# A two-block transformer kernel: the loop over further tiles goes to the very end, a shift's products beside an earlier stage, and a bias strip's copy behind the gates

## The chip, the cores and the metric

The kernel runs on one core of one Trainium2 chip. The metric is the device time of one execution in microseconds (us), as the median of several runs. The engines are TensorE (PE, with its weight loads as PEld), VectorE (DVE), ScalarE (ACT), GpSimd (POOL) and SyncE (SP), which issues most of the DMAs.

## The reference, cut to what matters

Two transformer blocks run one after the other on x (512 tokens, 1024 features). The parts that the change touches:

```
# first block
h = rms_norm(x, g_mix);  proj = h @ w_in             # conv, q, k, v, index, gates
y_a = short_conv_mixer(c_b, c_c, c_x) @ w_branch_a
logits = q k / 8 + rel_bias[rel_bucket(t - s)]       # the bias strip: 8 heads
merged = sigmoid(g_a) * y_a + sigmoid(g_b) * y_b
x = x + merged @ w_out
x = x + (silu(h2 @ w_ffn_gate) * (h2 @ w_ffn_up)) @ w_ffn_down
# second block
sh1, sc1, gt1, sh2, sc2, gt2 = split(silu(c) @ ada_w + ada_b)
h = rmsnorm(x, norm1_g) * (1 + sc1) + sh1            # sh1: the shift
z = h @ w_in                                         # first 768 columns: the latents
...
h = rmsnorm(x, norm2_g) * (1 + sc2) + sh2
x = x + gt2 * hierarchical_moe(h, ...)               # 32 experts, 2 of 8 in 1 of 4 groups
return rmsnorm(x, final_norm_g)
```

## The kernel before

Weights stream from HBM in blocks of 128 x 1024 (512 KB). `dense` (L351 on) loads a block on SP's queue (L333), splits it into a high part on ACT (L338) and a low part on POOL (L339), and multiplies on PE: three products per block of 128 features, high by high, high by low, low by high (L347). One output block takes 24 matmuls for 8 feature blocks, and 33 for the 11 feature blocks of a half of the down products. Nine buffers hold raw, high and low blocks. The order on each engine is made by a planner that simulates the program; a queue then works in that order. A `keep` pins an instruction to program order, and `issue_after` makes one wait for another.

First block. The index scores and the top-k (DVE, L566 and L567) run beside the convolution's products w_cv. A table `bd` of 8 x 640 biases is made (L598, written by ACT's queue) and spread into the strip `bt`, 8 x 128 x 512 values or 2 MB in DRAM, by one DMA (L645): each of the 128 rows is the table shifted by one. The strips `st` of the heads are fetched from bt in the attention (L766). Then come the gates: w_ga (sigmoid on ACT, L653), w_ya (times the gate, `mA`, on DVE, L660) and w_gb, whose rest is interleaved with the attention.

The feed-forward part runs in two halves. Each has 22 gate-up products (`w_gu`) and 8 down products (`w_dn`). Beside them the vectors of the second block are made: `ada` (L704) streams ada_w through DVE, one step a product in the first half, two in the second, where they run out after 12 of the 22 products. The latents' `shift` (six of them, one a product) loads a block of w_lat, multiplies it with the shift vector on DVE (L905, and seven times L907), sums over partitions by a product of one column on PE (L909) and copies it to `shc` (L910). They run beside the down products of the second half, as do the rotary tables and the masks.

The experts. Tokens are gathered into tiles; 16 tiles of two experts each are worked through in the order `seq`, and a 17th tile of 64 rows takes what did not fit. `finish` adds a tile's rows to `acc` in DRAM by an indirect DMA; the last two tiles (`NCH` = 2) stay on chip as `yh`, `yl` with one-hot matrices `oh`, and `place` adds them by products (L1799) to `fin`, the blocks read back from acc (L1789). If still more tiles are needed, `loop` works them one by one; their number `ntl` is data, and the loop runs from 1 to ntl, so for ntl = 1 it makes no pass. In the execution shown it makes none. It stands in the last step, after `hidden` of the 17th tile and before its `turn` and `finish`; at its place (L1730) every engine tests ntl, jumps, and then waits on the semaphores of all engines and queues before it goes on. At the end come the sums of squares (`sq`, ACT, L1821), the products with g (`tg`, POOL, L1824), the inverse root (`ms`, `rs`, DVE, L1825 and L413 to L421), the scaling and the output.

Of the kernel before, what the change touches and what calls it, by code (L numbers as in the profile page):

```python
# [11 lines left out]
F32 = mybir.dt.float32  # L12
F32R = mybir.dt.float32r
I32 = mybir.dt.int32
ACT = mybir.ActivationFunctionType
ALU = mybir.AluOpType
# [3 lines left out]
P = 128  # L20
S = 512
D = 1024
NB = 4
# [5 lines left out]
NL = 6  # L29
# [20 lines left out]
FM = "ppss"  # L50
# [23 lines left out]
GA1 = (0, 0, 0, 1, 0, 1, 0, 1, 1, 0)  # L74
NW = 9
NCH = 2
LOOP = 16
LF = True
NX = 18
NR = 8  # L80
# [5 lines left out]
AD = (1, 1, 2, 2)  # L86
# [152 lines left out]
def build(tc, A, out, taps=None):  # L239
    nc = tc.nc  # L240
# [11 lines left out]
    V, G = nc.vector, nc.gpsimd  # L252
    TT, STT, TS = V.tensor_tensor, V.scalar_tensor_tensor, V.tensor_scalar
    act = nc.scalar.activation
# [14 lines left out]
    def blk(name, dt=F32):  # L269
        if late:  # L270
            return late[0].tile([P, S], dt, tag="t", bufs=3, name=name)
        pool, tag = (lpool, "b") if name in LATE else (epool, "c") if name in EARLY else (epool, "d") if name in MID else (lpool, "t")
        return pool.tile([P, S], dt, tag=tag, bufs=BUFS[tag], name=name)

    def psum(tag, name=None):
        return psp.tile([P, S], F32, tag=tag, bufs={"mm": 3, "lg": 2, "tp": 2, "po": 1}[tag],
                        name="p" + (name or tag))

    def raw_tile(name="raw", dt=F32):
        return wpool.tile([P, D], dt, tag="w", bufs=NW, name=name)  # L280
# [50 lines left out]
    def wload(src, n):  # L331
        raw = raw_tile()
        nc.sync.dma_start(raw[:, :n], src)  # L333
        return raw
# [110 lines left out]
    class Ssq:  # L445
# [4 lines left out]
        def add(self, t, scale=1.0, pin=False):  # L450
            sq = blk("sq" if self.acc else "acc")
            i = act(sq, t, ACT.Square, scale=scale)
            if pin:
                keep(i)
            if self.acc is None:
                self.acc = sq
            else:
                self.eng.tensor_tensor(self.acc, self.acc, sq, ALU.add)
# [9 lines left out]
    def x_tile(name):  # L468
        return xpool.tile([P, D], F32, tag="x", bufs=4, name=name)
# [169 lines left out]
    def beside(i):  # L639
        scores.run(SC[3])  # L640
        if not scores.ts:
            tops.run(TOP)

    go(dense("w_cv", DB, h, ev_cv), beside)
    nc.sync.dma_start(bt, bass.AP(tensor=bd.tensor, offset=bd.offset + 127,  # L645
                                    ap=[[640, 8], [-1, P], [1, S]]))


    gts = {}
# [3 lines left out]
        act(t, ps, ACT.Sigmoid, bias=vcol("b_gate", m))  # L653
        gts[m] = t

    mA = []

    def ev_ya(m, ps):
        t = blk("mA")
        TT(t, ps, gts[m], ALU.mult)  # L660
        mA.append(t)

    ga, ya = dense("w_ga", DB, h, ev_ga), dense("w_ya", 4, chl, ev_ya)
    for _ in range(NGA):
        next(ga)
        tops.run(3)
        next(ya)
        tops.run(1)
    tops.run(99)

    gd = {}
# [227 lines left out]

    shc = kpool.tile([P, NL], F32, name="shc")  # L900

    def shift(c):
        raw = wload(A["w_lat"][c].rearrange("p m k c -> p (m k c)"), D)
        t = blk("t")[:, :P]
        TS(t, raw[:, :P], adac[:, :1], None, ALU.mult)  # L905
        for k in range(1, DB):
            STT(t, raw[:, k * P:(k + 1) * P], adac[:, k:k + 1], t, ALU.mult, ALU.add)  # L907
        ps = psum("lg", "shift")
        mm(ps[:, :1], t, one1[:, :1])  # L909
        act(shc[:, c:c + 1], ps[:, :1], ACT.Copy)  # L910

    shifts = Tasks(*[(shift, c) for c in range(NL)])


    gs1 = kpool.tile([P, 8], F32, name="gs1")
# [3 lines left out]
    for half in range(2):  # L919
        hid = []  # L920
        st = {}

        def ev_gu(m, ps):
            t = blk("t")
            if m % 2 == 0:
                TT(t, ps, r, ALU.mult)
                act(t, t, ACT.Silu)  # L927
                G.tensor_tensor(t, t, r, ALU.mult)  # L928
                st["g"] = t
            else:  # L930
                TT(t, ps, st["g"], ALU.mult)
                a = pair_of("h" if len(hid) < NH else "h1" if len(hid) < NH1 else "hid")
                split(t, *a)
                hid.append(a)

        if half == 0:
            with soon(1):
                r = rstd_of(ssq.done(), out=blk("m2"))
        if half == 0:
            keep(act(cact, vcol2("c", 0, 8), ACT.Silu))  # L940
            keep(G.tensor_copy(trib, cst[:, 256:384]))
            G.tensor_copy(tri2[:, :32], cst[:32, 256:288])
            G.tensor_tensor(tri2[:, 32:], cst[:32, 256:288], cst[:32, :32], ALU.add)
            G.tensor_copy(moeb, moec[:, 88:328])
            G.memset(oneb, 1.0)
        go(dense("w_gu", DB, h, ev_gu, src=A["w_gu"][half * 22:(half + 1) * 22]),
           lambda i: adas.run(AD[2 * half]))

        def ev_d(m, ps):
            TT(x[m], ps, x[m], ALU.add)  # L950
            if half:
                a = pair_of("xg")
                split(x[m], *a, scale=gs1[:, m:m + 1])
                xg.append(a)
                s1.add(x[m])
                s2.add(x[m], scale=vcol("g_final", m))

        if half:
            STT(gs1, adac[:, 8:16], 1.0, vcol2("norm1_g", 0, 8), ALU.add, ALU.mult)
            TT(gs1, gs1, vcol("g_final", 0, 8), ALU.mult)  # L960
            rt = rope_tables()
            mk = masks()
        go(dense("w_dn", 11, hid, ev_d, src=A["w_dn"][half]),
           lambda i: shifts.run(1) if half else adas.run(AD[2 * half + 1]))


    KQ = 96
# [719 lines left out]
    def weights(i, after=True):  # L1687
        g = seq[i]
        if g == 16:
            wes[i] = further(0)  # L1690
            return
        more(upto[g] - len(we), after)
        wes[i] = [[we[n, j] for j in range(3)] for n in (2 * g, 2 * g + 1)]
# [28 lines left out]
        ohs.append(oh)  # L1722
        ys.append((yh, yl))

    def loop():
        for j in range(LOOP + 1, 17):
            weights(j, LF)

        ntl = nc.values_load(ei[0:1, 16:17], min_val=1, max_val=16)
        with tc.For_i(1, ntl) as t:  # L1730
            st = mr[0].tile([P, 4], F32, name="lsl")[:, :3]

            nc.sync.dma_start(slots[16 * P:].rearrange("(g p) c -> p g c", p=P), slt[:, 16:])
            nc.sync.dma_start(st[:64], slots[bass.ds(16 * P + 64 * t, 64)])
            ix = mr[0].tile([P, 1], I32, name="lix")
            V.tensor_copy(ix[:64], st[:64, 0:1])
            w = further(t)
            xg = gather(xgb[0], ix, 64)
            scaled(64, xg, st)
            down(w, turned(64, hidden(w, features(64, xg, xtb), st)), yb[0])  # L1740
            add(64, yb[0], ix, acc)

    def rows_in_place(i):
        xts[i] = features(size(i), xgb[i % NQ], xtb)
# [16 lines left out]
    for i in range(17):  # L1761
        if i not in wes:
            weights(i)
        if i == 15:
            weights(16)
            gfr = xgb[i % NQ]
            keep(nc.sync.dma_start(gfr, A["gfin"].broadcast_to([P, D])))
        hss[i] = hidden(wes[i], xts.pop(i), slt[:, seq[i]], (lambda: turn(i - 1)) if i else None)
        if i < 16:
            rows_in_place(i + 1)  # L1770
        if i < 15:
            scaled(size(i + 2), xgb[(i + 2) % NQ], slt[:, seq[i + 2]])
        if i:
            finish(i - 1)
        if i == 0:
            further_tiles(further_slots())
        if i == LOOP:
            loop()
    turn(16)
    finish(16)  # L1780

    if LOOP == 17:
        loop()


    fin = []
    for b in range(NB):
        fin.append(mr[0].tile([P, D], F32, tag="we", bufs=NR, name="fin"))
        (nc.scalar if FQ and b % 2 else nc.sync).dma_start(fin[b], acc[b * P:(b + 1) * P])  # L1789
# [21 lines left out]
    for b in range(2):  # L1811
        for q in range(2):
            placed(b, q, 0)

    for g in FGR:
        n = len(g)
        ms = mr[0].tile([P, n], F32, tag="ms%d" % n, bufs=2, name="ms")
        tg = {}
        for j, b in enumerate(g):
            place(b)  # L1820
            act(x_tile("sq"), fin[b], ACT.Square, accum_out=ms[:, j:j + 1])  # L1821
            if FM[b] != "s":
                tg[b] = mr[0].tile([P, D], F32, tag="we", bufs=NR, name="tg")
                (G if FM[b] in "pq" else V).tensor_tensor(tg[b], fin[b], gfr, ALU.mult)  # L1824
        TS(ms, ms, 1.0 / D, EPS, ALU.mult, ALU.add)  # L1825
        r = rsqrt4(ms, lambda: mr[0].tile([P, n], F32, tag="rs%d" % n, bufs=6, name="rs"))
        for j, b in enumerate(g):
            t, c = fin[b], r[:, j:j + 1]
            if FM[b] == "s":
                STT(t, t, c, gfr, ALU.mult, ALU.mult)  # L1830
            elif FM[b] in "qw":
                t = tg[b]
                TS(t, t, c, None, ALU.mult)
            else:
                t = tg[b]
                act(t, t, ACT.Copy, scale=c)
            (nc.scalar if FQ and b % 2 else nc.sync).dma_start(out[b * P:(b + 1) * P], t)
# [16 lines left out]
```

## Time and profile before

| | |
|---|---|
| runs | 1366.8, 1363.75, 1368.21 us |
| median | 1366.8 us |
| profiled execution | 1365.68 us, of which the span from the first to the last instruction 1363.9 us |
| mean granted clock of TensorE | 0.964 |
| busy share | PE 93%, PEld 69%, DVE 62%, ACT 40%, POOL 47% |
| moved by DMA | 209.19 MB, 153 GB/s in the mean |

All rows come from one profiled execution. Its own time is the reference for sums of durations; the median of the runs is the reference for the result. A matmul's end is modelled: in the timeline the rows of PE overlap a little.

### The profile page before, as it was taken

How to read it: one execution, taken by the hardware profiler on the slowest of the kernel's cores; microseconds unless marked ns; L12 is line 12 of the kernel's file. 1: busy time of each engine (PE TensorE's matmuls, PEld its weight loads, DVE VectorE, ACT ScalarE, POOL GpSimd, SP SyncE). 2: the span in 40 equal slices, each digit the busy share in tenths (PEclk: the TensorE clock that was granted, in tenths of full speed). 3: DMA queues.
4: the chain of work that ended last, by engine and by line, in shares of the span. 5: the costliest groups of instructions: out<-in, count | busy, mean ns of one | idle time of the engine just before them, and what ended most of it. 6: DMA issues, size and time to landing. Idle time of an engine off the chain costs nothing. (4 is left out here: it accounts for less than half of the span.)

```text
span 1363.9 us, 16404 instructions
## 1 busy us (share of the span) xinstructions
PE 1263.6 (93%) x5818; PEld 946.5 (69%) x5818; DVE 845.9 (62%) x1490; ACT 544.8 (40%) x902; POOL 645.7 (47%) x365
## 2 busy tenths in 40 slices
PE   6798999999999999999998999899979999679985
PEld 5576887777888778777886777778855587445432
DVE  5857885543758443377249676979977753554424
ACT  4443236566333332222323454233376532244422
POOL 4514447454547554454745755346734263123311
PEclk9898999999999999999999999899989999879987
DMA  5214233223245544575333322234430069989983
GB/s 171 80 49 147 103 99 125 99 95 125 93 137 201 202 156 149 185 244 193 118 116 112 118 93 78 71 124 131 131 108 16 24 236 356 347 302 288 273 306 134
DMA packets 70403, 209.19 MB, mean 153 GB/s; under 512 B 9635, under 2 KB 14427, under 8 KB 70320
## 3 DMA queue, kind: packets, MB, share of 16 engines
q1 hardware_dynamic: 61456, 193.81, 41.4%
q0 software_dynamic: 4048, 8.01, 2.5%
q10 hardware_dynamic: 4816, 6.31, 1.3%
q8 instruction: 46, 0.75, 0.2%
q14 instruction: 37, 0.30, 0.1%
HBM read 195.06 MB, written 21.61 MB: 159 GB/s over the span
## 5 line engine op out<-in xcount | busy, mean ns | idle before, releaser
L339 POOL TENSOR_TENSOR wl<-raw,wh 128x1024 fp32r<-128x1024 f32 (+2 forms) x180 | 420.0, 2335 | 418.7 <-ACT wh L338 350.0
L338 ACT ACTIVATE wh<-raw 128x1024 fp32r<-128x1024 f32 (+2 forms) x183 | 183.3, 1003 | 297.8 <-DMA raw<-in_w_dn 59.3
L347 PE MATMUL pw_gu<-xg,wh 128*128 128x512 f32 x704 | 168.9, 391 | 0.0
L347 PEld LDWEIGHTS pw_gu<-xg,wh 128*128 128x128 f32 x704 | 131.4, 188 | 31.3 <-issue 2.5
L704 DVE SCALAR_TENSOR_TENSOR ad<-raw,cact,ad 128x512 f32<-128x512 f32 x84 | 89.0, 1107 | 37.1 <-DMA raw<-in_ada 37.1
L347 PE MATMUL pw_dn<-h,wh 128*128 128x512 f32 x352 | 88.6, 397 | 0.7 <-ACT wh L338 0.7
L347 PE MATMUL pw_cv<-h,wh 128*128 128x512 f32 x320 | 81.0, 405 | 8.0 <-ACT wh L338 5.0
L1048 DVE SCALAR_TENSOR_TENSOR ptaps<-u,vec,ptaps 128x511 f32<-128x511 f32 (+28 forms) x116 | 85.8, 739 | 3.6
L347 PE MATMUL pw_gu<-xg,wl 128*128 128x512 f32 x352 | 87.7, 390 | 0.0
L1639 PE MATMUL plg<-we,xt 128*64 128x256 f32 (+1 forms) x528 | 75.0, 406 | 9.2 <-DMA we<-in_we 6.0
L347 PEld LDWEIGHTS pw_cv<-h,wh 128*128 128x128 f32 x320 | 62.2, 196 | 23.6 <-ACT wh L338 5.9
L347 PEld LDWEIGHTS pw_dn<-h,wh 128*128 128x128 f32 x352 | 66.1, 190 | 15.6 <-ACT wh L338 1.2
L347 PEld LDWEIGHTS pw_gu<-xg,wl 128*128 128x128 f32 x352 | 65.9, 188 | 13.8
L1639 PEld LDWEIGHTS plg<-we,xt 128*64 128x64 f32 (+1 forms) x528 | 39.8, 136 | 40.2 <-issue 13.5
L347 PE MATMUL pw_gb<-h,wh 128*128 128x512 f32 x256 | 64.3, 394 | 0.0
L347 PE MATMUL pw_ga<-h,wh 128*128 128x512 f32 x256 | 62.3, 391 | 0.0
L347 PEld LDWEIGHTS pw_ga<-h,wh 128*128 128x128 f32 x256 | 47.7, 188 | 10.3 <-issue 0.8
L347 PEld LDWEIGHTS pw_gb<-h,wh 128*128 128x128 f32 x256 | 47.4, 188 | 9.2
L735 DVE TENSOR_SCALAR e<-e,ri 128x512 f32<-128x512 f32 (+2 forms) x64 | 49.0, 767 | 1.7
L928 POOL TENSOR_TENSOR t<-t,m 128x512 f32<-128x512 f32 x22 | 33.3, 1514 | 34.7 <-ACT t L927 32.7
L1600 POOL DMA_INDIRECT xg<-htok,sidx x17 | 17.2, 1012 | 67.2 <-ACT xt L1629 50.1
L733 ACT ACTIVATE e<-e,mx 128x512 f32<-128x512 f32 (+2 forms) x64 | 40.7, 637 | 20.1 <-DVE mx L776 13.2
(463 smaller groups left out, 2504.4 us busy)
## 6 DMA issues: line engine op xcount, KB each, us to landing
we<-in_we SPq DMA_DIRECT2D x99, 512.0 KB
raw<-in_ada SPq DMA_DIRECT2D x48, 512.0 KB
raw<-in_w_gu SPq DMA_DIRECT2D x44, 512.0 KB
raw<-in_w_cv SPq DMA_DIRECT2D x20, 512.0 KB
raw<-in_w_ga SPq DMA_DIRECT2D x16, 512.0 KB
raw<-in_w_gb SPq DMA_DIRECT2D x16, 512.0 KB
raw<-in_w_o SPq DMA_DIRECT2D x16, 512.0 KB
spill<-g SPq DMA_DIRECT2D x24, 256.0 KB
```

What stands on the lines that cost most here:

```text
L338: act(wh[:, :n], raw[:, :n], ACT.Copy)
L339: (eng or G).tensor_tensor(wl[:, :n], raw[:, :n], f(wh[:, :n]), ALU.subtract)
L347: mm(ps, w[:, o + k * M:o + (k + 1) * M], xs[k][i], start=(first and j == 0), stop=(last and j == n - 1))
L704: STT(t, raw[:, o], cact[:, k:k + 1], t, ALU.mult, ALU.add)
L733: act(e, e, ACT.Exp, scale=-1.0, bias=mx[:, h_, b:b + 1], accum_out=sm[:, h_, b:b + 1])
L735: (G if b in NP else V).tensor_scalar(e, e, r, None, ALU.mult)
L928: G.tensor_tensor(t, t, r, ALU.mult)
L1048: keep(STT((a if k else y)[:, s:], u[:, :S - s], w, a[:, s:], ALU.mult, ALU.add))
L1600: rows_in.append(keep(nc.gpsimd.indirect_dma_start(out=xg[:n], out_offset=None, in_=htok, in_offset=bass.IndirectOffsetOnAxis(ap=si_[:n], ...
L1639: keep(mm(pg[64 * j:min(64 * j + 64, n), :256], xt[:, k, 64 * j:min(64 * j + 64, n)], w[k // 4][:, k % 4 * 256:(k % 4 + 1) * 256], start=( ...
```

## The change

Four edits. The constant LOOP goes. The copy of the strip bt, with its DMA on SP's queue, goes from behind w_cv to behind the first four pairs of w_ga and w_ya products, and waits for the first mA. The shifts begin in the second half's gate-up products, one a product, once the ada steps are used up; each shift's small product and copy are issued one step later than its sums, so that there are seven steps for six shifts, and the tile t of the sums lives for two steps. The loop moves from the 17th step to behind the sums of squares and before the inverse root; its number ntl is read by all engines before fin is loaded; a pass no longer adds to acc in DRAM but places its rows on chip into fin and then makes the sums of squares and the products with g anew.

```
@@ first block @@
 go(dense("w_cv", DB, h, ev_cv), beside)
-nc.sync.dma_start(bt, bass.AP(tensor=bd.tensor, offset=bd.offset + 127,
-                                ap=[[640, 8], [-1, P], [1, S]]))
...
-mA = []
+mA, strip = [], []
 def ev_ya(m, ps):
     t = blk("mA")
-    TT(t, ps, gts[m], ALU.mult)
+    strip.append(TT(t, ps, gts[m], ALU.mult))
     mA.append(t)
...
     next(ya)
     tops.run(1)
+with tc.issue_after(strip[0].ins):
+    nc.sync.dma_start(bt, bass.AP(tensor=bd.tensor, offset=bd.offset + 127,
+                                    ap=[[640, 8], [-1, P], [1, S]]))
 tops.run(99)
@@ shifts @@
+sht = {}
 def shift(c):
+    if c > 0:
+        ps = psum("lg", "shift")
+        mm(ps[:, :1], sht[c - 1], one1[:, :1])
+        act(shc[:, c - 1:c], ps[:, :1], ACT.Copy)
+    if c == NL:
+        return
     raw = wload(A["w_lat"][c].rearrange("p m k c -> p (m k c)"), D)
-    t = blk("t")[:, :P]
+    t = sht[c] = blk("t")[:, :P]
     TS(t, raw[:, :P], adac[:, :1], None, ALU.mult)
     for k in range(1, DB):
         STT(t, raw[:, k * P:(k + 1) * P], adac[:, k:k + 1], t, ALU.mult, ALU.add)
-    ps = psum("lg", "shift")
-    mm(ps[:, :1], t, one1[:, :1])
-    act(shc[:, c:c + 1], ps[:, :1], ACT.Copy)
-shifts = Tasks(*[(shift, c) for c in range(NL)])
+shifts = Tasks(*[(shift, c) for c in range(NL + 1)])
...
     go(dense("w_gu", DB, h, ev_gu, src=A["w_gu"][half * 22:(half + 1) * 22]),
-       lambda i: adas.run(AD[2 * half]))
+       lambda i: adas.run(AD[2 * half]) if adas.ts else shifts.run(1))
...
     go(dense("w_dn", 11, hid, ev_d, src=A["w_dn"][half]),
-       lambda i: shifts.run(1) if half else adas.run(AD[2 * half + 1]))
+       lambda i: None if half else adas.run(AD[1]))
@@ loop @@
-def loop():
-    for j in range(LOOP + 1, 17):
-        weights(j, LF)
-    ntl = nc.values_load(ei[0:1, 16:17], min_val=1, max_val=16)
+def loop(ntl, ms, tg):
     with tc.For_i(1, ntl) as t:
...
         down(w, turned(64, hidden(w, features(64, xg, xtb), st)), yb[0])
-        add(64, yb[0], ix, acc)
+        yh, yl, oh = raw_tile("yh", F32R), raw_tile("yl", F32R), raw_tile("oh", F32R)[:, :S]
+        for b in range(NB):
+            TS(oh[:64, b * P:(b + 1) * P], it128[:64], float(P * b), st[:64, 0:1], ALU.add, ALU.is_equal)
+        for q in range(2):
+            o = slice(q * S, (q + 1) * S)
+            split(yb[0][:64, o], yh[:64, o], yl[:64, o])
+        for b in range(NB):
+            for q in range(2):
+                o, ps = slice(q * S, (q + 1) * S), psum("mm")
+                for i, y in enumerate((yh, yl)):
+                    mm(ps, oh[:64, b * P:(b + 1) * P], y[:64, o], start=(i == 0), stop=(i == 1))
+                TT(fin[b][:, o], ps, fin[b][:, o], ALU.add)
+            sums(b, ms, tg)
...
-    if i == LOOP:
-        loop()
...
 fin = []
+ntl = nc.values_load(ei[0:1, 16:17], min_val=1, max_val=16)
...
+def sums(b, ms, tg):
+    act(x_tile("sq"), fin[b], ACT.Square, accum_out=ms[:, b:b + 1])
+    if b in tg:
+        (G if FM[b] in "pq" else V).tensor_tensor(tg[b], fin[b], gfr, ALU.mult)
 for g in FGR:
     ms = mr[0].tile([P, n], F32, tag="ms%d" % n, bufs=2, name="ms")
+    tg = {b: mr[0].tile([P, D], F32, tag="we", bufs=NR, name="tg") for b in g if FM[b] != "s"}
     for b in g:
         place(b)
+        sums(b, ms, tg)
+    loop(ntl, ms, tg)
     TS(ms, ms, 1.0 / D, EPS, ALU.mult, ALU.add)
```

## Rows read from the trace of the kernel before

**Rows 1.** The page: the span, and PE's busy us, share, instructions.

```profile
span 1363.9 us, 16404 instructions
...
PE 1263.6 (93%) x5818; PEld 946.5 (69%) x5818; DVE 845.9 (62%) x1490; ACT 544.8 (40%) x902; POOL 645.7 (47%) x365
```

**Rows 2.** Waits of SP's own queue, 85 to 135 us.

```profile
SPq L645 <- DMA bd<-bs: 21.8, 1, 21.8
```

**Rows 3.** Timeline of SP, 85 to 135 us: start, us, what.

```profile
95.73 0.79 SPq L645 DMA_DIRECT2D bt<-bd  x1
96.64 38.23 SPq L333 DMA_DIRECT2D raw<-in_w_cv  x8
```

**Rows 4.** Timeline of ACT, 105 to 115 us; in brackets the idle time before.

```profile
110.18 1.06 ACT L338 ACTIVATE wh<-raw 128x1024 fp32r<-128x1024 f32 x1 [4.47 <-DMA raw<-in_w_cv]
```

**Rows 5.** Timeline of PE, 85 to 135 us.

```profile
111.28 5.99 PE L347 MATMUL pw_cv<-h,wh 128*128 128x512 f32 x16 [4.79 <-ACT wh L338]
...
119.41 3.79 PE L347 MATMUL pw_cv<-h,wh 128*128 128x512 f32 x16
...
124.85 3.79 PE L347 MATMUL pw_cv<-h,wh 128*128 128x512 f32 x16
```

**Rows 6.** Waits of PE, whole span: total us, times, longest us.

```profile
PE pshift L909 <- DVE t L907: 7.3, 5, 3.4
```

**Rows 7.** Timeline of PE, 700 to 800 us: the stage's first row, the next stage's.

```profile
703.11 2.88 PE L347 MATMUL pw_dn<-h,wh 128*128 128x512 f32 x12
...
778.07 0.39 PE L373 MATMUL pw_lat<-xg,wh 128*128 128x512 f32 x1
```

**Rows 8.** Windows: stretch, length, busy by engine, granted clock, DMA share, GB/s.

```profile
720.00:740.00 20.00, 15.43 (x62) 11.59 (x61) 19.93 (x35) 7.80 (x14) 9.57 (x7) 0.92 0.31 101
740.00:760.00 20.00, 18.33 (x80) 14.27 (x78) 19.47 (x24) 7.01 (x13) 14.83 (x10) 0.99 0.46 143
760.00:780.00 20.00, 17.81 (x72) 14.31 (x73) 12.19 (x15) 8.42 (x14) 15.29 (x9) 0.91 0.30 101
...
600.00:620.00 20.00, 18.40 (x78) 13.64 (x77) 15.71 (x18) 6.10 (x9) 10.47 (x5) 1.00 0.71 242
```

**Rows 9.** Groups of instructions, 703 to 780 us: busy us, mean ns, idle before.

```profile
L907 DVE SCALAR_TENSOR_TENSOR t<-raw,adac,t 128x128 f32<-128x128 f32 x42 | 29.7, 728 | 0.9
```

**Rows 10.** Timeline of DVE, 1332 to 1346 us.

```profile
1337.17 0.69 DVE L1668 TENSOR_TENSOR y<-pmm,gt2r 112x512 f32<-112x512 f32 x1 [2.18 <-ACT yh L308]
```

**Rows 11.** Timeline of PE, 1330 to 1342 us.

```profile
1338.04 3.43 PE L1667 MATMUL pmm<-we,ht 128*64 128x512 f32 x4 [0.64 <-DVE ht L1658]
```

**Rows 12.** Windows of 1 us, columns as in rows 8.

```profile
1339.00:1340.00 1.00, 1.00 (x3) 0.38 (x2) 0.96 (x3) 0.00 (x0) 0.00 (x0) 0.50 0.98 385
```

**Rows 13.** Timeline of SP, 172 to 215 us.

```profile
185.23 0.33 SPq L333 DMA_DIRECT2D raw<-in_w_ga  x1
189.42 12.04 SPq L333 DMA_DIRECT2D raw<-in_w_gb  x3
201.56 0.38 SPq L766 DMA_DIRECT2D st<-bt  x1
```

**Rows 14.** Timeline of ACT, 176 to 210 us: a split of weights.

```profile
188.76 1.06 ACT L338 ACTIVATE wh<-raw 128x1024 fp32r<-128x1024 f32 x1 [6.04 <-DMA raw<-in_w_ga]
```

**Rows 15.** Timeline of DVE, 184 to 187 us: the first mA.

```profile
185.76 0.67 DVE L660 TENSOR_TENSOR mA<-pw_ya,g 128x512 f32<-128x512 f32 x1
```

**Rows 16.** Timeline of PE, 172 to 215 us: where these weights are used.

```profile
198.29 3.79 PE L347 MATMUL pw_ga<-h,wh 128*128 128x512 f32 x16
...
206.45 3.79 PE L347 MATMUL pw_gb<-h,wh 128*128 128x512 f32 x16
```

**Rows 17.** One line, L907: ns min, median, max of one instruction.

```profile
L907 DVE SCALAR_TENSOR_TENSOR t<-raw,adac,t x42: 338/352/1932, 728.1 to 769.8; 128x128 f32<-128x128 f32 x42
```

**Rows 18.** Timeline of DVE, 1342 to 1356 us: last addition, and the scaling.

```profile
1350.89 0.69 DVE L1809 TENSOR_TENSOR fin<-pmm,fin 128x512 f32<-128x512 f32 x1 [0.63 <-PE pmm L1799]
1352.84 0.17 DVE L1825 TENSOR_SCALAR ms<-ms 128x4 f32<-128x4 f32 x1 [1.26 <-ACT sq L1821]
```

## What I expect, and why

> **What bounds the kernel now.** The page comes first. TensorE (PE) works in 93% of the span [rows 1], so a change pays if it removes a stretch in which PE stands, or one in which PE runs at half clock because it stood. The table of waits, cut to PE, names such stretches; in it I look for lines that the diff touches. The table is not an account of the end, because a wait early in the kernel counts only if PE stays the bound behind it. It does: all of PE's idle time together is 1363.9 - 1263.6 = 100 us [rows 1], spread over many places.
>
> First place: the strip of biases. SyncE's queue stood 21.8 us before the strip's copy, waiting for the landing of the table bd that ScalarE writes [rows 2]; the copy went out at 95.73 and the next weight load of w_cv stands right behind it [rows 3]. That load reached ScalarE's split only at 110.18 [rows 4]; PE had run dry and stood 4.79 us, and the sixteen products after the wait took 5.99 us where the same sixteen take 3.79 at full clock [rows 5].
>
> Second place: the shift's share. Within the down products of the second half PE waited 7.3 us in five waits for the last vector instruction of a shift [rows 6]. The stage runs from 703.11 to 778.07, 74.96 us [rows 7]. Its 8 x 33 products at the cadence of [rows 5] ((124.85 - 119.41) / 24 = 0.2267 us each) would take 59.85 us, so 15.1 us are excess. The windows split them: PE idle 4.57 + 1.67 + 2.19 = 8.4 us, and a granted clock of 0.92, 0.99 and 0.91, short by 1.6 + 0.2 + 1.8 = 3.6 us [rows 8]; the remaining 3.1 I put to the twelve small products of the shifts and to restarts. VectorE (DVE) is full there (19.93 and 19.47 of 20): it holds the 42 multiply-adds, which take 728 ns each in the mean [rows 9].
>
> Third place: the loop. It runs no pass in this execution, yet at its place every engine checks all semaphores. DVE's second half of y stood 2.18 us behind it [rows 10]. PE's next four products took 3.43 us [rows 11], at a granted clock of 0.50, the lower of its two levels [rows 12].
>
> **The change, part by part.**
>
> *Strip, removal.* The load of w_cv no longer has a 2 MB copy in front of it. A weight load issued at 185.23 is split at 188.76, 3.5 us later [rows 13, 14]; so the load of about 96.6 would be ready near 100, or a few us later if its buffer is late, and PE needs it at 111.28 - 4.79 = 106.5. Gain: 4.79 + (5.99 - 3.79) = 7.0 us; from below 0, if the load's buffer is the later one. I take 7.0, since the copy is the only thing in the queue that differs from the other loads.
>
> *Strip, addition.* The copy now waits for the first mA, which ends at 186.4 [rows 15], where SyncE has just issued a load (185.23) and issues the next at 189.42 [rows 13]; SyncE loses about 1 us at the head of its queue. Behind it the copy competes with the loads of w_gb. In the old place the load issued behind the copy was ready 110.18 - 95.73 = 14.5 us after it; the same delay here puts the first w_gb at 186.4 + 14.5 = 200.9, and PE takes it at 206.45 [rows 16]. Cover 5.5 us, cost 0. The strips are first fetched at 201.56 [rows 13], by the same measure just after the copy's end. If the planner puts the copy ahead of the load of 185.23, that load is ready at 200.9 and PE wants it at 198.29 [rows 16]: 2.6 us idle, and about as much again for the clock. Bounds 0 and 5; I take 0. With PE earlier by 7, all of these times move together.
>
> *Shift.* Six loads of 512 KB, 48 vector instructions, twelve small products and six copies move from the 33-product steps of the down stage into 24-product steps of the gate-up stage, after the last ada step; the product of one shift is now issued one step after its sums. Removed from the down stage: 15.1 less 1.1 (idle that the shift did not cause, 8.4 - 7.3) less about 2 for the products, which move and cost the same: 12 us. Added: a step lasts 24 x 0.2267 = 5.44 us; a shift has eight vector instructions, 2.8 us at their undisturbed 0.35 [rows 17] and 5.8 at the mean of the down stage. The nearest work is the ada stretch of the same stage: four larger instructions a step, DVE at 15.71 of 20, PE still at 18.40 of 20, the last of the windows in [rows 8]. So I put 2 us of new PE waits over the six steps, bounds 0 and 6 x 0.4 (the excess of 5.8 over 5.44) plus the clock, about 6. The DMA queue has room there: one weight load a step is left once the ada loads end. Net +10, bounds +6 and +12.
>
> The spread between 338 and 1932 ns for one and the same instruction [rows 17] I read as the price of GpSimd working beside it. The Trainium skill (GPSIMD Engine Reference, "Key points") says that GpSimd shares its SBUF interfaces with VectorE and contends with vector instructions that have two SBUF inputs; these multiply-adds have two, the trace agrees, and the rule speaks against the new place, where GpSimd splits a weight in every step. By it alone, with every instruction at 728 ns, the 2 us would be the 6 of the upper bound, and the sum 4 us less.
>
> *Loop.* At the old place 2.18 us of DVE go, and with them the half clock of the four products (up to 1.7 of their 3.43); y of the last pair then follows without a stop. I take 2.7, bounds 2.2 and 3.9. At the new place the check stands between the last sum of squares and the scaling. DVE's last addition ends at 1351.58, and its 1.26 us of idle before the scaling [rows 18] hide part of the same 2.18: 0.9 us remain; 2.2 if the check starts only after ScalarE is done. The longer body changes nothing while no pass runs, except that the jump is longer: -2 as an outer bound, the size of one such wait. Net +1.8, bounds -2 (2.2 - 2.2 - 2) and +3 (3.9 - 0.9).
>
> Sum: 7.0 + 10 + 1.8 = 18.8 us. The profiled execution took 1365.7 us (span 1363.9), so 1346.9; the median of the runs is 1.1 above it, and against that the forecast is **1348.0 us**. Its own range is 1342 (7 + 12 + 3 = 22, and the 3 us by which the fastest run shown lies under the median) to 1353 (5 + 8 + 1 = 14).
>
> **The rivals.**
>
> 1. *The strip's stall moves behind the gates.* For it: the copy and one load still take up to 14.5 us, and loads still queue behind it; if it slips before the load of 185.23, the price is the 5 us above. Against it: the load of 185.23 is split by 189.82, 8.5 us before PE wants it [rows 14, 16]. Then the strip gives 2, the sum is 13.8, the time 1353.
>
> 2. *The shift's waits come along by half.* For it: the steps are shorter by 9 products, and GpSimd is busy in half of the ada stretch (10.47 of 20). Against it: ada's steps in the same place. Then the shift gives 4, the sum is 12.8, the time 1354.
>
> 3. *Slower: the shift stalls PE more than before.* Place: the small product in PE's queue between two gate-up products. In the down stage a step of 7.48 us covered a shift; here 5.44 do, 2.04 less, six times: 12.2 us on top of the 7.3, and at half clock behind each wait about 7 more, together 26 against the 12 saved. The shift then costs 14, the time is 1366.8 - 7 - 1.8 + 14 = 1372. It decides from 21 us of such waits on; below, the change stays faster. Against it: the product now has a whole step's delay.
>
> 4. *Nothing reaches the end.* The order on each engine comes from a planner over the whole program; a moved step can shift other work, and new stalls of 15 to 20 us eat the gain: 1366, within 0.3% (4 us, about what a measurement of this kernel can tell from no change). Nothing in the profile shows such a place.
>
> **How the numbers follow.** Forecast 0.63, rival 1 0.15, rival 2 0.12, rival 3 0.05, rival 4 0.05. Faster takes the first three, 0.90; same 0.05; slower 0.05. The range for 8 in 10 runs from the forecast's lower end, 1342, over rivals 1 and 2 to 1357, where both together (18.8 - 5 - 6 = 7.8) come near 1359.
>
> **What would show it.** Right: no wait on bd in SyncE's queue, PE without a gap and at clock 1.00 between the first and second w_cv product; the down stage of the second half near 62 us; PE still full through the gate-up stage; behind the last pair no stop of 2 us, and one of about 1 us more before the scaling. Wrong: ScalarE waiting for a w_ga or w_gb load that PE wants; waits of PE on the shift's sums between gate-up products; a loop check longer than 2.2 us at the end; or a loss of PE time in the first attention, where the strips arrive.

## The result, and the profile after

Before: 1367.8 us, the median of 9 runs (1363.75 to 1369.59). After: 1357.83 us, 9 runs (1354.07 to 1362.33). The ratio is 0.9931, with a 95% interval of 0.9915 to 0.9948: about 10 us faster, where 18.8 were forecast. The time lies above the range of 1342 to 1357.

The page of the kernel after (span; busy time of each engine, as in [rows 1]):

```profile
span 1352.3 us, 16401 instructions
...
PE 1260.2 (93%) x5818; PEld 946.4 (70%) x5818; DVE 842.9 (62%) x1490; ACT 545.0 (40%) x902; POOL 644.6 (48%) x365
```

The span is 11.6 us shorter; the profiled execution after, of 1354.07 us, is the fastest of its nine, so the 10.0 us between the medians are the surer figure. Where the span is shorter is read stage by stage: from the timeline of PE, the distance from the first product of a stage to the first product of the next. The stages between those listed differ by at most 0.6 us.

| stage (us) | before | after | change |
|---|---|---|---|
| up to the first w_cv product | 97.44 | 98.23 | +0.8 |
| w_cv, first block | 76.37 | 76.71 | +0.3 |
| w_ga up to the end of w_o (gates, attention, output) | 215.69 | 215.69 | 0 |
| w_gu, second half | 127.33 | 130.87 | +3.5 |
| w_dn, second half | 74.97 | 59.84 | -15.1 |
| w_cv, second block | 61.36 | 59.05 | -2.3 |
| experts, to the end of the last placing product | 170.54 | 170.71 | +0.2 |
| from there to the end | 13.03 | 13.87 | +0.8 |

The strip first. The kernel after has the same rows as the kernel before ([rows 2 to 5]). The waits of SP's queue (a q behind an engine's name stands for its sequencer, which issues and waits):

```profile
SPq L667 <- DMA bd<-bs: 21.8, 1, 21.8
```

The timelines of SP, of ACT and of PE:

```profile
96.53 0.79 SPq L667 DMA_DIRECT2D bt<-bd  x1
97.44 34.55 SPq L332 DMA_DIRECT2D raw<-in_w_cv  x7
...
110.97 1.06 ACT L337 ACTIVATE wh<-raw 128x1024 fp32r<-128x1024 f32 x1 [4.46 <-DMA raw<-in_w_cv]
...
112.07 6.32 PE L346 MATMUL pw_cv<-h,wh 128*128 128x512 f32 x16 [4.78 <-ACT wh L337]
```

The copy of bt goes out at 96.53, some 90 us before the first mA (186.91) for which it was to wait, and still stands in front of a load of w_cv. ACT's split and PE's stop behind it are there as before.

The shift ([rows 6 to 9]). PE's waits:

```profile
PE pshift L908 <- DVE t L916: 1.8, 1, 1.8
```

The windows, with the columns of [rows 8]: two of the gate-up products, one of all the down products:

```profile
660.00:680.00 20.00, 20.00 (x92) 16.63 (x91) 18.36 (x30) 5.25 (x9) 10.38 (x5) 1.00 0.50 171
680.00:707.80 27.80, 26.01 (x118) 21.27 (x117) 15.00 (x23) 9.67 (x15) 19.10 (x10) 1.00 0.29 94
707.80:767.60 59.80, 59.80 (x265) 49.55 (x264) 36.50 (x46) 26.44 (x39) 43.41 (x27) 1.00 0.35 112
```

The shift's multiply-adds in the groups of lines:

```profile
L916 DVE SCALAR_TENSOR_TENSOR t<-raw,adac,t 128x128 f32<-128x128 f32 x42 | 27.6, 658 | 1.3
```

The rows show that the down stage is full at clock 1.00 over its whole length: 59.84 us, the 59.85 that its products take at full cadence. In the gate-up stage PE stops once, for 1.79 us. The multiply-adds take 658 ns in the mean, hardly less than in the old place (728), and they did not hold PE up more than that. The mean hides two kinds: 34 of the 42 take under 0.5 us, and eight take 1.26 to 2.45, each with GpSimd at work for at least 88% of its time; in the old place there were 13 such slow ones, 1.25 to 1.93 us long.

The end ([rows 10, 11, 18]). DVE's timeline before, the two rows that go with those of [rows 10]: the first half of y of the last pair, and the copy of ht, right behind the second half.

```profile
1334.30 0.69 DVE L1668 TENSOR_TENSOR y<-pmm,gt2r 112x512 f32<-112x512 f32 x1 [0.25 <-PE pmm L1667]
...
1337.78 0.21 DVE L1658 COPY ht<-ptp 128x64 f32<-128x64 f32 x1
```

After, the timelines of DVE and PE at this place, and DVE at the new place of the loop:

```profile
1321.90 1.52 DVE L1674 TENSOR_TENSOR y<-pmm,gt2r 112x512 f32<-112x512 f32 x2 [0.25 <-PE pmm L1673]
1323.34 0.68 DVE L308 TENSOR_TENSOR yl<-y,yh 112x512 fp32r<-112x512 f32 x1
1323.94 0.86 DVE L1722 TENSOR_SCALAR oh<-moeb,slt 64x128 fp32r<-64x128 bf16 x4
1324.72 0.68 DVE L308 TENSOR_TENSOR yl<-y,yh 112x512 fp32r<-112x512 f32 x1
1325.33 0.21 DVE L1664 COPY ht<-ptp 128x64 f32<-128x64 f32 x1
...
1325.59 3.58 PE L1673 MATMUL pmm<-we,ht 128*64 128x512 f32 x4 [1.01 <-DVE ht L1664]
...
1341.28 0.17 DVE L1840 TENSOR_SCALAR ms<-ms 128x4 f32<-128x4 f32 x1 [2.15 <-ACTq L1733]
```

The two halves of y now follow without the stop of 2.18 us. But ht, which PE's next four products need, stands behind yl, oh and yl; before, it came right behind the second y. From the first y to the start of the four products it was 1338.04 - 1334.30 = 3.74 us [rows 11], and it is 1325.59 - 1321.90 = 3.69. The four products still take 3.58 us, at a granted clock of 0.53 over their stretch. Before the scaling DVE now stands 2.15 us in place of 1.26.

### The profile page after: what moved, and what is told of

Its sections match the earlier page's. It is cut to its first block, busy times and chain, and to the rows that moved or that the text cites. A ratio compares the mean times of both kernels' runs of the same rounds, so it can differ in the third digit from the quotient of the medians.

```text
span 1352.3 us, 16401 instructions
## 1 busy us (share of the span) xinstructions
PE 1260.2 (93%) x5818; PEld 946.4 (70%) x5818; DVE 842.9 (62%) x1490; ACT 545.0 (40%) x902; POOL 644.6 (48%) x365
## 5 line engine op out<-in xcount | busy, mean ns | idle before, releaser
L346 PE MATMUL pw_dn<-h,wh 128*128 128x512 f32 x352 | 85.4, 390 | 0.0
L346 PEld LDWEIGHTS pw_dn<-h,wh 128*128 128x128 f32 x352 | 65.9, 188 | 14.5 <-issue 0.8
L1606 POOL DMA_INDIRECT xg<-htok,sidx x17 | 17.2, 1011 | 69.1 <-ACT xt L1635 49.7
```

The lines of the kernel that those rows point to most:

```text
L346: mm(ps, w[:, o + k * M:o + (k + 1) * M], xs[k][i], start=(first and j == 0), stop=(last and j == n - 1))
L1606: rows_in.append(keep(nc.gpsimd.indirect_dma_start(out=xg[:n], out_offset=None, in_=htok, in_offset=bass.IndirectOffsetOnAxis(ap=si_[:n], ...
```

## The experiments

One table for all of them: stage lengths as above, in us of one profiled execution, then the median, and the ratio to the runs of the kernel before on the same chip. The kernels ran on several chips, so their ratios are compared and not their medians. The experts' column also moves between kernels with the same loop: from the first product of the routing to the first y of the last pair it takes 150.9 (e12_bound_top) to 156.3 us (e1_bound) with the loop at its new place, and 153.3 to 154.0 with it at the old. The loop is therefore read from that y to the last addition into fin.

| kernel | w_cv | w_ga to w_gb | w_gu, 2nd half | w_dn, 2nd half | experts | to the end | median | ratio (95%) |
|---|---|---|---|---|---|---|---|---|
| before | 76.37 | 32.64 | 127.33 | 74.97 | 170.54 | 13.03 | 1367.8 | |
| after | 76.71 | 32.64 | 130.87 | 59.84 | 170.71 | 13.87 | 1357.83 | 0.9931 (0.9915 to 0.9948) |
| e4_strip | 76.95 | 32.64 | 127.35 | 75.57 | 170.02 | 13.03 | 1368.24 | 1.0005 (0.9990 to 1.0020) |
| e1_bound | 68.59 | 35.91 | 133.61 | 59.84 | 170.82 | 13.80 | 1356.4 | 0.9913 (0.9891 to 0.9935) |
| e6_act | 69.71 | 32.64 | 130.91 | 59.84 | 171.15 | 13.87 | 1349.92 | 0.9863 (0.9838 to 0.9887) |
| e7_top | 69.74 | 32.64 | 133.07 | 59.84 | 170.72 | 13.84 | 1347.83 | 0.9847 (0.9823 to 0.9872) |
| e12_bound_top | 68.62 | 32.64 | 133.87 | 59.84 | 169.14 | 13.83 | 1347.79 | 0.9857 (0.9834 to 0.9881) |
| e10_act_only | 69.71 | 32.64 | 127.35 | 74.07 | 170.41 | 13.02 | 1363.19 | 0.9955 (0.9939 to 0.9972) |
| e2_shift | 77.08 | 32.64 | 130.77 | 59.84 | 170.02 | 12.71 | 1356.05 | 0.9926 (0.9899 to 0.9953) |
| e8_nodefer | 77.02 | 32.64 | 132.97 | 59.84 | 169.24 | 13.87 | 1360.41 | 0.9928 (0.9900 to 0.9957) |
| e3_loop | 77.19 | 32.64 | 127.35 | 75.55 | 169.16 | 14.00 | 1368.44 | 1.0014 (0.9998 to 1.0029) |
| e5_order | 76.28 | 32.64 | 130.77 | 59.84 | 168.00 | 13.86 | 1353.75 | 0.9901 (0.9873 to 0.9928) |
| e9_both | 69.73 | 32.64 | 130.77 | 59.84 | 167.12 | 13.86 | 1348.77 | 0.9863 (0.9839 to 0.9887) |
| e11_no_loop | 69.74 | 32.64 | 133.03 | 59.84 | 170.00 | 12.94 | 1347.85 | 0.9833 (0.9806 to 0.9861) |

### The strip

**e4_strip**: the kernel before with the strip's edit alone, as the diff above makes it.

> The kernel before with the strip's edit alone, as the change makes it (tied to the first mA). Theory A: nothing moves; SyncE issues the copy at about 96 us, right behind the landing of the table, PE's gap of 4.8 us inside w_cv stays, and the time is that of before within 0.2%. Rival (the forecast): the copy goes out behind the first mA, near 180 us, w_cv is 7 us shorter, 1361 us.

The timelines of SP and PE (PE's window ends within its row, which shows the first six products):

```profile
100.04 0.79 SPq L668 DMA_DIRECT2D bt<-bd  x1
...
115.64 2.93 PE L347 MATMUL pw_cv<-h,wh 128*128 128x512 f32 x6 [4.84 <-ACT wh L338]
```

The copy goes out at 100.04 (the whole start of this execution is 4.3 us later, see the last section), 1.7 us before the first w_cv product, and the stop is 4.84 us. The edit by itself moves nothing.

**e1_bound**: the tie to an instruction of SP's own queue.

```diff
+loads = []
 def wload(src, n):
     raw = raw_tile()
-    nc.sync.dma_start(raw[:, :n], src)
+    loads.append(nc.sync.dma_start(raw[:, :n], src))
...
-with tc.issue_after(strip[0].ins):
+with tc.issue_after(loads[-1].ins):
```

> The changed kernel, with the strip's copy tied to the last weight load traced ahead of it (an instruction of SyncE's own queue) and no longer to the first mA (an instruction of VectorE). Theory A: in the changed kernel the copy never moved, because the tie to an instruction of another engine orders nothing; the stall it causes is still there and is worth what was forecast. Then the copy goes out behind the loads of w_ga, PE's gap of 4.8 us inside w_cv and the half clock behind it go, the stage w_cv falls from 76.9 to about 70 us, and the kernel is 5 to 7 us faster than the changed one: 1351 to 1353 us against 1357.8. Rival B: the load behind the copy was late for its buffer, not for the copy; the gap stays and so does the time, 1357.8. Rival C: the stall moves with the copy to w_gb: w_cv is 7 us shorter and the gates and the attention up to 5 us longer, 1355 to 1356.

Now the copy moves, and w_cv is full and 8.1 us shorter than in the kernel after. But 3.3 us are given back between the first w_ga and the first w_gb product. The timelines of ACT, PE and SP, in order of time:

```profile
170.50 0.72 ACT L629 ACTIVATE t<-u,vec 128x512 f32<-128x512 f32 x1 [6.84 <-DVE u L626]
...
176.12 1.17 PE L348 MATMUL pw_ga<-h,wh 128*128 128x512 f32 x4 [1.68 <-ACT wh L339]
...
179.21 0.50 PE L348 MATMUL pw_ya<-cv,wh 128*128 128x512 f32 x1 [1.00 <-DVE cv L308]
...
182.58 0.80 SPq L669 DMA_DIRECT2D bt<-bd  x1
```

ACT's waits from 150 to 200 us:

```profile
ACT t L629 <- DVE u L626: 14.6, 2, 7.8
```

The window 130 to 150 us, with the columns of [rows 8] (DVE is the third engine):

```profile
130.00:150.00 20.00, 20.00 (x90) 16.56 (x89) 19.66 (x46) 5.50 (x7) 10.14 (x4) 1.00 0.31 101
```

PE's two stops, at 176 and 179, end before the copy goes out at 182.58; the copy can't be their cause. Read backward: PE's stop at 176 waits for a split of ACT (175.08), this for POOL's low part of the split before it (172.26 to 175.05), that split (171.13) stands in ACT's queue behind t, which waited 6.84 us for u of DVE, and DVE is busy for 19.66 of 20 us. The stop at 179 waits for DVE itself. With its stall gone, w_cv is short enough that DVE, with the top-k and the convolution, comes last. Behind the first w_gb product this kernel is 5.8 us longer than the kernel after, 2.7 of them in the second gate-up stage; e7_top, with no copy behind the gates, is 3.4 us longer there, 2.2 of them in the same stage (the last section has it).

**e6_act**: the copy on ACT's queue, right behind the table, and nothing behind the gates.

```diff
 bt = dram.tile([8, P, S], F32, name="bt")
+nc.scalar.dma_start(bt, bass.AP(tensor=bd.tensor, offset=bd.offset + 127, ap=[[640, 8], [-1, P], [1, S]]))
...
-with tc.issue_after(strip[0].ins):
-    nc.sync.dma_start(bt, ...)
```

> The changed kernel, with the strip's copy issued by ScalarE's queue right behind the table, so that SyncE's loads run ahead as in e1_bound, but no copy stands behind the gates. Theory A: what e1_bound lost in the gates (5.2 us) came from VectorE, which is behind with the top-k when w_cv runs without its stall; then w_cv is 68 to 70 us here too, and the stretch of the gates and the attention is again 4 to 5 us longer, the time 1354 to 1357 us. Rival B: the moved copy caused the loss, by its transfer beside the loads of w_gb; then that stretch is 215.7 us as in the changed kernel, and the time 1350 to 1352 us.

Timelines of SP, of ACT's queue and of PE (first products of w_cv and of w_ga; the windows end within these rows):

```profile
78.02 50.65 SPq L332 DMA_DIRECT2D raw<-in_w_cv  x8
...
98.61 0.55 ACTq L597 DMA_DIRECT2D bd<-bs  x1
...
100.63 0.75 ACTq L599 DMA_DIRECT2D bt<-bd  x1
...
101.91 1.43 PE L346 MATMUL pw_cv<-h,wh 128*128 128x512 f32 x5 [0.21 <-ACT wh L337]
...
171.62 1.75 PE L346 MATMUL pw_ga<-h,wh 128*128 128x512 f32 x7
```

w_cv takes 69.71 us, 7.0 less than after, and the gates lose nothing. The same 2 MB copy, at the same time, costs nothing when it does not stand in the loads' queue: its place in SP's queue was the price. In the kernel after SP issues no load of weights between 74.36 and 97.44; here two of the eight go out in that time, at 88.12 and 96.85. How much of the stop came from this wait, and how much from the transfer, beside which the next load then ran, was not taken apart. The gates' loss of e1_bound stays away too, as rival B had it; but the mechanism of rival B is contradicted by the order of times above, so one more pair was needed.

**e7_top** and **e12_bound_top**: `TOP = 2` in place of 3 (top-k steps beside one w_cv product), once on e6_act, once on e1_bound.

> e6_act with two top-k steps beside each w_cv product in place of three, the rest of them in the gates, where the changed kernel works them too. Theory A (VectorE is behind at the end of w_cv): the stops of TensorE at the first w_ga and w_ya products go, and part of the 5 us of the gates comes back, 1350 to 1354 us. Rival B (the copy or the buffers cause the loss): as e6_act, or slower, because the masks of the attention come later.

> e1_bound (the copy on SyncE's queue, behind the loads of w_ga) with two top-k steps beside each w_cv product in place of three. Theory A: the two stops at the first w_ga and w_ya products came from VectorE, which ran behind; with a third of its top-k taken out of w_cv they go, the stretch from the first w_ga to the first w_gb product falls from 35.9 to 32.6 us, and the copy costs no more than 0.5 us behind it: time 1349 to 1353 us. Rival B: the copy's place is the cause; then the stretch stays at 35 us or more and the time at 1355 to 1357 us.

On e6_act the edit changes nothing in w_cv and in the gates (69.74 and 32.64): DVE was not late there. On e1_bound the two stops go (35.91 to 32.64). The timelines of PE and SP of e12_bound_top:

```profile
170.34 3.79 PE L348 MATMUL pw_ga<-h,wh 128*128 128x512 f32 x16
173.97 1.98 PE L348 MATMUL pw_ga<-h,wl 128*128 128x512 f32 x8
175.78 1.98 PE L348 MATMUL pw_ya<-cv,wh 128*128 128x512 f32 x8
...
181.75 0.80 SPq L669 DMA_DIRECT2D bt<-bd  x1
```

ACT's waits from 150 to 200 us:

```profile
ACT t L629 <- DVE u L626: 6.4, 2, 3.3
```

The copy is in the same place as in e1_bound, the wait for u has fallen from 14.6 to 6.4 us, and PE has no stop. So DVE's lateness was the cause. Why DVE is late in e1_bound and not in e6_act, which has the same three steps, goes with its instructions: the convolution's eight multiply-adds (t<-u,vec,t) take 1.27 us each in the mean in e1_bound and 0.75 in e6_act. What stretches them there was not tested. Behind the copy, from the first w_gb product to the first w_yb product, it takes 112.96 us against 111.68: placed as the change meant it, the copy costs 1.3 us. (Gates, attention and output as a whole take 2.2 us more than after; e11_no_loop, with no copy there, takes 1.5 more.)

**e10_act_only**: the kernel before with the copy on ACT's queue and no other edit.

> The kernel before with one edit: the strip's copy goes out on ScalarE's queue right behind the table, not on SyncE's. Theory: the price of the strip's stall is the forecast's 7.0 us, whatever the rest of the change does; w_cv falls from 76.4 to 69.7 us, the gates and the attention stay at 215.7, time 1360 to 1362 us. Rival: part of the gain of e6_act comes from the shift or the loop; then less than 5 us.

w_cv falls from 76.37 to 69.71 us, and by the runs the gain is 0.45% of 1369.76 us, the median of the kernel before on that chip: 6.2 us. The price of the stall does not depend on the other edits.

### The shift

**e2_shift**: the kernel before with the shift's edit alone, as in the diff above.

> The kernel before with the shift's edit alone. Theory A: the shift carries the whole gain. The second half's down stage falls from 75.0 to about 60 us, its gate-up stage rises from 127.3 to about 131, the latents' w_cv stage of the second block falls by about 2; together 11 to 14 us less than before, 1354 to 1357 us. Rival: part of the gain belongs to the loop, as forecast; then the shift alone gives no more than 8 to 10 us, 1358 to 1360 us.

The window of its down stage:

```profile
711.00:771.00 60.00, 60.00 (x266) 49.68 (x265) 36.32 (x47) 26.45 (x39) 43.72 (x27) 1.00 0.34 111
```

PE's waits:

```profile
PE pshift L908 <- DVE t L916: 1.7, 1, 1.7
```

The gate-up and down stages are within 0.1 us those of the kernel after, and so is w_cv of the second block (58.95; in e3_loop and e4_strip, without the shift's edit, 61.31 and 61.35). The ratio, 0.9926, is that of the whole change: the shift carries all of it.

**e8_nodefer**: the small product back in the step of its sums.

```diff
-    if c > 0:
-        ps = psum("lg", "shift")
-        mm(ps[:, :1], sht[c - 1], one1[:, :1])
-        act(shc[:, c - 1:c], ps[:, :1], ACT.Copy)
-    if c == NL: return
...
+    ps = psum("lg", "shift")
+    mm(ps[:, :1], t, one1[:, :1])
+    act(shc[:, c:c + 1], ps[:, :1], ACT.Copy)
```

> The changed kernel, with each shift's small product in the same step as its sums again. Theory A: the place alone makes the gain; the planner puts the product late in the step anyway, and TensorE waits no more than 2 to 4 us for sums in the whole stage: time within 2 us of the changed kernel's 1357.8. Rival B: the later product is what keeps TensorE from waiting; without it there are four to six waits of about 1 us each in the gate-up stage, with half clock behind some, 5 to 10 us more, 1363 to 1368 us.

PE's waits:

```profile
PE pshift L911 <- DVE t L909: 2.3, 1, 2.3
```

The window that holds it:

```profile
690.00:715.00 25.00, 22.75 (x96) 18.36 (x95) 11.06 (x19) 7.01 (x11) 14.87 (x9) 0.93 0.30 96
```

One wait of 2.25 us in place of 1.79; the stage is 2.1 us longer, mostly by the clock (0.93 over 25 us is 1.7 us). Kernels with the later product show the same length (e7_top 133.07). The place makes the gain; the later product, which I held against rival 3, is not what decides.

### The loop

**e3_loop**: the kernel before with the loop's edit alone, as in the diff above.

> The kernel before with the loop's edit alone. Theory A: at the old place nothing is gained, because the planner orders VectorE anew there and the last transposed tile now waits for three splits in place of the loop's check; at the new place 0.9 us are lost. From the first y of the last pair but one to the last addition into fin 17.2 us as before, from there to the scaling 0.9 us more; time 0.5 to 1.5 us above that of before. Rival (the forecast): 1.8 us faster, the stretch from that y to the last addition 2.2 to 3.9 us shorter.

DVE's timeline shows the order of the kernel after:

```profile
1337.75 1.52 DVE L1667 TENSOR_TENSOR y<-pmm,gt2r 112x512 f32<-112x512 f32 x2 [0.26 <-PE pmm L1666]
...
1341.18 0.21 DVE L1657 COPY ht<-ptp 128x64 f32<-128x64 f32 x1
```

From the first y to the last addition into fin it takes 16.9 us, 0.4 less than before (17.3; after: 17.2), and the tail is 1.0 us longer. In the seven kernels with the loop's edit and the planner's order this stretch is 15.3 to 19.0 us long, in the four with the loop at its old place 17.3 to 17.4. By the runs the edit alone is worth nothing: ratio 1.0014, interval 0.9998 to 1.0029.

**e5_order**: the kernel after, with `turn(16)` ahead of the splits, and the splits and one-hot matrices of DVE tied to its copy (an instruction of DVE itself).

```diff
     down(wes.pop(i), hts.pop(i), y)
+    if i == 15:
+        turn(16)
+    with tc.issue_after(copies[-1].ins):
         (one-hot matrices and splits)
...
-turn(16)
 finish(16)
```

> The changed kernel, with the transposed tile ht of the 17th tile put ahead of the splits yl and the one-hot matrices on VectorE. Theory A: at the old place the loop's check had cost 2.2 us, and the planner's new order, in which ht waits behind yl, oh and yl, gave all of it back; then with ht first the stretch from the first y of the last pair to the last addition into fin falls from 17.2 to about 15 us, and the time by 1.5 to 2.5 us, to 1355.5 us. Rival B: the stretch is bound elsewhere (the second splits, or the placing products); then it stays at 17 us and the time at 1357.8.

Timelines of DVE and PE:

```profile
1320.40 1.53 DVE L1676 TENSOR_TENSOR y<-pmm,gt2r 112x512 f32<-112x512 f32 x2 [0.25 <-PE pmm L1675]
1321.84 0.21 DVE L1666 COPY ht<-ptp 128x64 f32<-128x64 f32 x1
...
1322.11 1.93 PE L1675 MATMUL pmm<-we,ht 128*64 128x512 f32 x4 [0.73 <-DVE ht L1666]
```

The four products start 1.7 us after the first y, not 3.7, and take 1.93 us, not 3.58. From the first y to the last addition (it ends at 1334.89) it is 14.5 us, 2.7 less than after, and 14.5 again in e9_both and e11_no_loop. That is the size of the price that the prediction had given to the old place of the loop. It is shown by this stretch: the runs (0.9901 against 0.9931, the intervals overlap) do not tell it from nothing.

**e11_no_loop**: e9_both (below) without the loop; the work of further tiles is left out, of which there is none here.

> e9_both without the loop over further tiles (the work of further tiles, of which this input has none, is left out). It shows what the loop still costs at the end: 0.9 us between the last sum of squares and the scaling by the forecast, so the stretch from the last placing product to the end falls from 13.9 to about 13.0 us. Rival: the check costs the full 2.2 us there, or reading ntl and the longer program cost more than the check; then 11.7 us or less.

DVE's timeline at the scaling:

```profile
1338.55 0.17 DVE L1841 TENSOR_SCALAR ms<-ms 128x4 f32<-128x4 f32 x1 [1.26 <-ACT sq L1830]
```

1.26 us of idle again, not 2.13 as in e9_both, and a tail of 12.94 us, not 13.86: the check costs 0.9 us at its new place. The experts' 170.00 us, 2.9 above e9_both, lie ahead of the last pair (156.2 and 153.4 us to its first y).

### Both repairs

**e9_both**: e6_act and e5_order together.

> The changed kernel with both repairs: the strip's copy from ScalarE's queue (e6_act) and ht ahead of the splits (e5_order). If the two prices are separate, the stage w_cv stays near 69.7 us, the stretch of the experts near 168.0, and the time is 7 + 2.7 us below the changed kernel: 1347 to 1349 us, a ratio to the kernel before of 0.983 to 0.987. If the end of the experts is bound by the expert weights' loads, the second part gives nothing and it is 1350 us as e6_act.

The prices add up in the trace: w_cv 69.73, experts 167.12, span 1344.8 us. Its median, 1348.77 us, beats both kernels; by its runs it can't be told from e6_act (0.9863 both), so the second repair is seen in the trace alone. e7_top and e12_bound_top, with the strip moved and the smaller TOP but without the second repair, came out as low. e5's repair on e12_bound_top was not tried.

## Why the prediction was wrong

**The strip (forecast +7.0; got -0.3).** This is the step that failed: "*Strip, addition.* The copy now waits for the first mA", and with it "the load of w_cv no longer has a 2 MB copy in front of it". I took the line `issue_after` for a wait of any instruction on any other, as the kernel's description above says. It held the copy back only when it named an instruction of the copy's own queue (e1_bound), not when it named one of DVE (e4_strip). Nothing in the trace of before could show that, but its code gave a hint: each of its three uses names an instruction of the engine that it holds back; "the edit does nothing" was not among the rivals for this part, and rival 4 covered it only for the whole change. The price itself was right: 7.0 us in e6_act and 6.7 in e10_act_only by w_cv's length, 6.2 by the runs of the latter. Placed as meant, the copy costs 1.3 us (e12_bound_top; bounds 0 and 5, I took 0), and rival 1's loss, 5 us, did not come. What came in its place in e1_bound I had not named: DVE became the last one.

**The shift (forecast +10, bounds 6 and 12; got 11.6).** The mechanism is right, and the size within its bounds. Of the down stage all 15.1 us of excess went, not 12: the 1.1 us of other waits went with the shift too. The gate-up stage got 3.5 us more: one wait of 1.79 (forecast 2) and 1.75 besides. By the distances between the products around them the twelve small products are some 1.1 of these 1.75 (2.2 in the old place; I had let them move at about 2); the rest has no place that I know. Outside of my sum, the second block's w_cv gained 2.3 us: PE's idle time at its beginning falls from three stops, together 3.0 us, with a clock of 0.91 over the first 20 us, to one of 2.11 at 1.00. It goes with the shift's edit (e2_shift); what of the shift delayed that stage was not taken apart, and in four of the other kernels with this edit the gain is 1.2 to 1.3 us (last section). Rivals 2 and 3 did not happen. The prediction's rule, from the Trainium skill (GPSIMD Engine Reference, "Key points"), that GpSimd contends with vector instructions of two SBUF inputs, would have cost 4 us; the trace agrees with the slow instructions (eight of 42, all beside GpSimd's work), not with the cost, since PE waited but once.

**The loop (forecast +1.8; got -1.0).** The new place costs 0.84 us in the tail (forecast 0.9; 0.9 by e11_no_loop). At the old place 2.7 us were forecast and none came (from the first y to the last addition 17.3 us before, 17.2 after; the experts as a whole +0.2). The stop of 2.18 us did go; the step that failed is "and with them the half clock of the four products": I had the products follow y, and they follow ht, which the planner now puts behind two splits and the one-hot matrices. In e5_order the 2.7 us are there. So the mechanism of rival 4, a planner that shifts other work, did happen in this one place, at 2.7 us and not its 15 to 20.

Sum: -0.3 + 11.6 + 2.3 - 1.0 = 12.6, less 0.8 in the start and some 0.2 elsewhere, which no edit touches: the 11.6 us between the two spans. The medians differ by 10.0. With the two parts that did not take effect made to do so, e9_both runs at 1348.8 us; the forecast was 1348.0. That they are so close is in part luck: in e9_both's trace the shift gives 1.7 us more than forecast and the second block's w_cv 1.2 that were in no sum, while its start is 3.0 us longer than before.

## What to carry to other kernels

Before a moved step is priced, make sure that it moves: look for what holds it in the order of its own queue, and give "it stays" a chance of its own. A stop that is taken off one engine pays only if the instruction that the bound engine needs next moves up; where a planner orders anew, name that instruction and check its place. A DMA's place in a queue can be its price: the same 2 MB copy cost 7 us in the loads' queue and nothing in another.

## What the hardware showed that was not expected

The start, up to the first w_cv product, has the same work in all these kernels, and its length is 97.2 to 101.9 us. Two of them are e5_order (97.48) and e6_act (101.91). PE's timeline in e5_order, and then its window 25 to 30 us:

```profile
24.54 0.50 PE L373 MATMUL pw_qk<-xg,wh 128*128 128x512 f32 x1 [2.14 <-DVE xg L311]
```

```profile
25.00:30.00 5.00, 5.00 (x28) 4.21 (x27) 3.42 (x16) 0.00 (x0) 0.00 (x0) 1.00 0.27 97
```

The same two of e6_act:

```profile
24.48 0.50 PE L373 MATMUL pw_qk<-xg,wh 128*128 128x512 f32 x1 [2.38 <-DVE xg L311]
```

```profile
25.00:30.00 5.00, 5.00 (x19) 4.25 (x19) 2.22 (x8) 0.00 (x0) 0.00 (x0) 0.59 0.26 97
```

After the stop of 2.14 us the granted clock stays at 1.00; after the one of 2.38 us it is 0.59 in the mean of 5 us, towards the lower level of 1.2 GHz, with 19 products in the window where there were 28. PE's next stop, 1.54 us in both, ends at 35.94 and at 39.06: 3.1 of the 4.4 us by which the two executions are apart at the first w_cv product.

The length of a stop does not by itself tell which way it goes. At this place a stop of 2.34 us in e11_no_loop is followed by a clock of 1.00 from 25 to 30 us, one of 2.25 us in e3_loop by 0.70. At the beginning of the second block's w_cv all ten kernels with the shift's edit have the same stop of 2.11 us: in six of them the clock over the stage's first 20 us is 1.00 and the stage takes 59.0 us, in four (e1_bound, e6_act, e8_nodefer, e9_both) it is 0.91 and the stage takes 60.0 to 60.2. What decides it is not known from these runs.

In the gate-up stage of the second half the two groups lie apart: where PE's stop for the shift is 1.67 to 1.79 us long, the stage takes 130.8 to 130.9 us; where it is 2.25 to 2.75 us long, 133.0 to 133.9. Half a microsecond more of stop went with two to three of time there. So differences below some 4 us between two executions of these kernels are read from the stage that was edited, not from the span.
